# A two-block mixture-of-experts network on one core: tokens gathered from x in fp32 with scaled one-hot columns, expert sums in another slot, and a pair's products in a new order

## The chip, the cores and the metric

The kernel runs on one core of a Trainium2 chip. The metric is the device time of one execution in microseconds (us); lower is better. The core has a matrix engine (TensorE, PE in the profile, with PEld for the loading of its stationary operand), a vector engine (VectorE, DVE), a scalar engine (ScalarE, ACT), GpSimd (POOL), and SyncE (SP), whose queue issues the transfers of weights from HBM into SBUF.

## What is computed

256 tokens of 1024 features go through three layers. Each is a mixer (attention and a recurrence, of different kinds), whose result is added to x, and then a mixture of experts: a router picks a group and two of its eight experts for each token, of 32 in all, and the experts' results are added to x. The change is in the mixture of experts. Cut to what matters, with the grouping of rows left out:

```python
def _hier_moe(h, w_group, b_group, w_expert, b_expert, w1, w3, w2):
    g_sel = jnp.argmax(g_logits, axis=-1)
    top_v, top_i = lax.top_k(e_in, MOE_TOPK)
    gate = (p_g * jax.nn.softmax(top_v, axis=-1)).reshape(-1)
    ids = (g_sel[:, None] * MOE_EXPERTS_PER_GROUP + top_i).reshape(-1)
    ...
    def expert_block(args):
        tok, e = args
        xr = xt[tok]
        return (jax.nn.silu(xr @ w1[e]) * (xr @ w3[e])) @ w2[e]
    ...
    out = jax.ops.segment_sum(y * w_row[:, None], seg, num_segments=N + 1)[:N]

# in the block
h = _rms(x, norm2_w[layer]) * (1 + scale2) + shift2
x = x + gate2 * _hier_moe(h, ...)
```

## The kernel before

x lies in SBUF as two tiles of 128 tokens (NT = 2) by 1024 features in fp32. Feature p*8+k belongs to the k-th of KC = 8 groups, so that `x[:, t].rearrange("q (p k) -> q k p")` reads one group at a step of eight elements.

All weights come through a ring of 19 slots of 1 MB. `plan` queues a weight, `pump` issues its transfer on SyncE as soon as a slot is free beyond a reserve, `done` and `release` give slots back. Parts of the kernel take slots of this ring for themselves: `out_last` (L520), the end of each mixer, takes one for hT, the turned tokens that the router's logits read, and two (hh and hl, L525) for the tokens times their rms factor r, as a high and a low part in fp32r. `token_high` (L557, ScalarE) makes the high part, one operation of 128x1024 per tile, and `token_low` (L561, VectorE) the low part, in halves. At the start of `moe`, hT's slot is given back.

`moe` (L1791) works through 16 pairs of experts, each expert with room for 64 tokens. The program is recorded in the order in which it is written; each engine runs its own instructions in that order and waits on semaphores for the others.

- `onehot(j)` (L1808): for two pairs, u = 1 where a token's rank is a column's number (VectorE).
- `gather(j)` (L1820): xg = the tokens of two pairs. 32 products with hh and hl as the stationary operand and u as the moving one, 256 columns wide; for the first two pairs it is done in two halves of 128 columns. The results leave PSUM by `affine`, by turns on ScalarE and VectorE.
- `gather_w(p)` (L1833): turns the weighted one-hots uw on TensorE; pg and ws are made of them on VectorE.
- `up(p, "g")` and `up(p, "u")` (L1844): 16 products each of xg with the weights. The first ends in sg (ScalarE), the second in hh, the tile of that name in `moe` (VectorE, L1861).
- `turn(p)` (L1866): hh is turned on TensorE, and copied to ht by VectorE (L251).
- `down(p)` (L1889): 16 products of ht with the weights; the result is split in yh and yl.
- `combine(p, t)` (L1902): yh and yl times pg, and VectorE adds the result to x.

Pair p combines the pair before it: one half between up g and up u, the other after the turn. Odd pairs gather for the next two pairs after up u, except pair 5 (LATE), which does so after its down products and combines itself at once. A branch there (`overflow`, L1740) is for experts with more tokens than room, and isn't taken with these inputs. Products that the trace shows twice per instruction are those in fp32.

Of the kernel before, what the change touches and what calls it, by code (L numbers as in the profile page):

```python
# [9 lines left out]
FT = mybir.dt.float32  # L10
# [4 lines left out]
OP = mybir.AluOpType  # L15
# [107 lines left out]
class Net:  # L123
# [396 lines left out]
    def out_last(self, act, gate):  # L520
        got = []
        setup = self.route_setup()
        next(setup)
        self.hT = self.slot().rearrange("p (k q) -> p k q", k=KC)
        self.hs = [self.slot(FR).rearrange("p (t k q) -> p t k q", t=NT, k=KC) for i in range(2)]  # L525
        self.hr = self.cp.tile([P, NT], FT, name="xr", bufs=2)
        for t in range(NT):
            for n in range(2):
                p = self.psum()
                for k2 in range(2):  # L530
                    i = 2 * n + k2
                    if i == len(got):
                        self.prep()
                        got.append(self.ready.pop(0))
                    wh, wl = got[i]
                    for k in range(2):
                        kk = 2 * k2 + k
                        self.mm3(p, tuple(x[:, P * t:P * t + P] for x in act[kk]), (wh[:, k], wl[:, k]), kk == 0, kk == 3)
                    yield (1.3, 0.0)
                self.out_sink(t, n, gate, True)(p)  # L540
                if not t and not n:
                    next(setup)
                if n and not t:
                    self.token_rstd(0)
                    self.token_high(0)
                if t:
                    (self.route_logits if n else self.route_turn)(0)
                    self.token_low(0, 4 * n)
                    yield (1.8, 0.0)
        self.token_rstd(1)  # L550

    def token_rstd(self, t):
        r = self.hr[:, t:t + 1]
        self.nc.vector.tensor_reduce(r, self.ssq[:, t, :2], axis=AX.X, op=OP.add)
        self.rstd(r, r, D)

    def token_high(self, t):  # L557
        xv = self.x[:, t].rearrange("q (p k) -> q k p", k=KC)
        self.nc.scalar.activation(self.hs[0][:, t], xv, AF.Copy, scale=self.hr[:, t:t + 1])

    def token_low(self, t, k):  # L561
        xv = self.x[:, t].rearrange("q (p k) -> q k p", k=KC)
        hh, hl = self.hs
        self.nc.vector.scalar_tensor_tensor(hl[:, t, k:k + 4], xv[:, k:k + 4], self.hr[:, t:t + 1],
                                            hh[:, t, k:k + 4].bitcast(FT), op0=OP.mult, op1=OP.subtract)

    def plan_cols(self, key, w, c0, n):
        src = w.rearrange("(p k) n -> p k n", k=KC)[:, :, c0:c0 + n]
# [1087 lines left out]
    def route(self, g, r, mods, rest):  # L1656
        nc = self.nc
        lg = g.tile([P, NT, 36], FT, name="lg")
        for t in range(NT):
# [34 lines left out]
        rest()  # L1694
# [42 lines left out]
        for i in range(n):  # L1737
            self.mm(p[:, :476], self.ident, self.km, True, True)

    def overflow(self, g, l, h, rk, wt, ti, w1, w3, w2, gate):  # L1740
        nc, tc = self.nc, self.tc
        rv = nc.values_load(ti, min_val=0, max_val=T, skip_runtime_bounds_check_because="rank < T")
        with tc.If(rv >= CAP):  # L1743
# [3 lines left out]
            cnt = g.tile([P, 1], FT, name="top")  # L1747
            nc.vector.memset(cnt, 0.0)
            hT = g.tile([P, KC, T], FT, name="xg")
            for t in range(NT):  # L1750
                for k0 in (0, 4):
                    p = self.psum().rearrange("d (k q) -> d k q", k=4)
                    for k in range(4):
                        for i, part in enumerate(h):
                            self.mm(p[:, k], part[:, t, k0 + k].bitcast(FT), self.ident, i == 0, i == 1)
                    for k in range(4):
                        self.affine(hT[:, k0 + k, P * t:P * t + P], p[:, k], k0 + k, "v")
            with tc.For_i(0, E, 1) as e:
# [7 lines left out]
                with tc.For_i(0, 4, 1) as c:  # L1766
# [12 lines left out]
                    for t in range(NT):  # L1779
                        for n in range(2):  # L1780
                            sl = slice(512 * n, 512 * n + 512)
                            p = self.psum()
                            self.mm(p, ho[:, P * t:P * t + P], wt_[:, sl], True, True)
                            tmp = g.tile([P, 512], FT, name="sg", bufs=2)
                            nc.vector.tensor_scalar(tmp, p, wc[:, t:t + 1], None, op0=OP.mult)
                            if gate:
                                nc.vector.tensor_mul(tmp, tmp, self.ga[:, sl])
                            xs = self.x[:, t, sl]
                            nc.vector.tensor_add(xs, xs, tmp)

    def moe(self, l, mods, start, coeffs, slots, fill=None):  # L1791
        nc, tc = self.nc, self.tc
        _, w1, w3, w2, gate = self.moe_args(l)
        with tc.tile_pool(name="moe", bufs=1, reuse_waits="tile") as g:
            hh, hl = self.hs
            r = self.hr
            self.route_turn(1)
            self.token_high(1)
            self.route_logits(1)
            self.release()  # L1800
            rk, wt, ti, finish, late = self.route(g, r, mods, lambda: self.token_low(1, 0))
            NP = E // 2
            st = {}
            if l == 2:
# [1 line left out]
            bc = lambda a, e, n: a[:, :, e:e + n, None].to_broadcast([P, NT, n, CAP])  # L1806

            def onehot(j):  # L1808
                u = g.tile([P, NT, 4, CAP], FR, name="u", bufs=2)
                nc.vector.tensor_tensor(u, self.iota[:, None, None, :].to_broadcast([P, NT, 4, CAP]), bc(rk, 4 * j, 4),  # L1810
                                        op=OP.is_equal)
                st["u", j] = u

            def weighted(p):
                uw = g.tile([P, NT, 2, CAP], FT, name="uw")
                u = st["u", p // 2][:, :, p % 2 * 2:p % 2 * 2 + 2].bitcast(FT)
                nc.vector.tensor_mul(uw, u, bc(wt, 2 * p, 2))
                st["uw", p] = uw

            def gather(j, c=slice(0, 2 * P)):  # L1820
                if c.start == 0:
                    st["xg"] = g.tile([P, KC, 2 * P], FT, name="xg")
                xg = st["xg"]
                u = st["u", j].rearrange("p t a s -> p t (a s)")
                for k0 in range(0, KC, 2):
                    ps = self.psum().rearrange("p (k s) -> p k s", k=2)[:, :, :c.stop - c.start]
                    for k in range(2):
                        for t in range(NT):
                            for i, part in enumerate((hh, hl)):
                                self.mm(ps[:, k], part[:, t, k0 + k], u[:, t, c], t + i == 0, t + i == 2)  # L1830
                    for k in range(2):
                        self.affine(xg[:, k0 + k, c], ps[:, k], k0 + k, "av"[k])

# [32 lines left out]
            def turn(p):  # L1866
                ps = self.psum()
                for k in range(4):
                    self.tr(ps[:, P * k:P * k + P], st["hh", p][:, k])
                ht = g.tile([P, 512], FT, name="ht").rearrange("p (k s) -> p k s", k=4)  # L1870
                self.copy(ht, ps.rearrange("p (k s) -> p k s", k=4), "v")
                st["ht", p] = ht

            def parts(p, sl, ps):
# [73 lines left out]
            for p in range(NP):  # L1948
                last = p == NP - 1
                if last:  # L1950
                    self.reserve += max(0, slots - 2)
                    if l == 2:
                        fo = self.slot().rearrange("p (t d) -> p t d", t=NT)
                else:
# [27 lines left out]
                (down_last if last else down)(p)  # L1982
                if p == LATE:
                    combine(p, 0)
                    combine(p, 1)
                    self.overflow(g, l, (hh, hl), rk, wt, ti, w1, w3, w2, gate)
                    gather(p // 2 + 1)
                if p == NP - 2:
                    coeffs()
# [81 lines left out]
```

## Time and profile before

| | before |
|---|---|
| median of three runs | 2085.38 us (2081.81 to 2085.57) |
| profiled execution | 2082.4 us, of which the span is 2080.6 us |
| mean granted clock of TensorE | 0.972 |
| TensorE busy | 1885.0 us, 91% |
| weight loads (overlap the products) | 1039.9 us, 50% |
| VectorE busy | 859.2 us, 41% |
| ScalarE busy | 431.3 us, 21% |

The span is one execution, taken by the hardware profiler. The three MoE layers lie at about 228 to 690, 869 to 1331 and 1621 to 2071 us of it; between them lie the mixers. Busy shares are means over stages with different limits. In a row of a group of instructions, `ps<-u,slot 128*128 128x256 f32 x32` means: written tile, read tiles, size of the stationary operand, size of the moving one, and how many.

### The profile page before, as it was taken

Reading aid. Unit: us, or ns where it says so; the run is one execution under the profiler, and the core shown is the slowest. Engines: PE = TensorE matmul, PEld = TensorE weight load, DVE = VectorE, ACT = ScalarE, POOL = GpSimd, SP = SyncE. Lnnn points to the kernel's source line nnn. Section 1 sums busy time; section 2 is a strip of 40 time slices with the busy share of each in tenths; the row PEclk is TensorE's granted clock in tenths of the full one; section 3 lists DMA queues with packets and bytes.
Section 4 is the critical chain, followed back from the end, with each engine's and each line's share of the span. In section 5 each row is a group of like instructions: output and inputs, shape, how many; then the busy total and the mean of one; then the engine's idle time right before and its main releaser. Section 6 shows DMA issues by size and latency. Waiting matters only on the chain. (4 is left out here: it accounts for less than half of the span.)

```text
span 2080.6 us, 25139 instructions
## 1 busy us (share of the span) xinstructions
PE 1885.0 (91%) x10032; PEld 1039.9 (50%) x10032; DVE 859.2 (41%) x1601; ACT 431.3 (21%) x790; POOL 309.6 (15%) x245
## 2 busy tenths in 40 slices
PE   5898899899999889899999999998899999899997
PEld 3656444434444657544343444586788444344443
DVE  3665433323332657633223332367666332222223
ACT  1423211111010333311010111244543111001111
POOL 1331000000000424100000000143443000000000
PEclk8997999999999999999999999899999999999999
DMA  9696999999999966799999999931357999999997
GB/s 322 258 304 236 363 422 422 420 421 421 421 421 406 343 214 247 303 391 421 421 420 421 421 421 421 337 111 41 123 191 270 373 421 421 420 421 421 421 421 270
DMA packets 157542, 725.30 MB, mean 349 GB/s; under 512 B 25305, under 2 KB 43087, under 8 KB 85225
## 3 DMA queue, kind: packets, MB, share of 16 engines
q1 hardware_dynamic: 139216, 716.84, 86.0%
q10 hardware_dynamic: 18201, 6.76, 1.3%
q8 instruction: 82, 1.34, 0.3%
q14 instruction: 43, 0.35, 0.0%
HBM read 722.48 MB, written 1.07 MB: 348 GB/s over the span
## 5 line engine op out<-in xcount | busy, mean ns | idle before, releaser
L258 PE MATMUL ps<-slot,xg 128*64 128x512 f32 x2952 | 680.9, 598 | 0.0
L258 PEld LDWEIGHTS ps<-slot,xg 128*64 128x64 f32 x2952 | 231.0, 138 | 408.7 <-issue 391.7
L258 PE MATMUL ps<-slot,ht 128*64 128x512 f32 (+1 forms) x1592 | 344.8, 574 | 67.6 <-issue 62.9
L258 PE MATMUL ps<-slot 128*128 128x256 f32 (+8 forms) x2230 | 369.9, 326 | 14.0 <-DVE slot L462 9.6
L258 PEld LDWEIGHTS ps<-slot 128*128 128x128 f32 (+3 forms) x2230 | 300.4, 186 | 74.0 <-issue 16.0
L258 PEld LDWEIGHTS ps<-slot,ht 128*64 128x64 f32 x1592 | 130.3, 138 | 257.0 <-issue 244.3
L1908 DVE TENSOR_TENSOR x<-x,ps 128x512 f32<-128x512 f32 x180 | 115.2, 681 | 246.1 <-PE ps L258 246.1
L1882 POOL TENSOR_TENSOR yl<-sg,yh 128x512 fp32r<-128x512 f32 (+1 forms) x68 | 82.4, 1212 | 870.8 <-ACT yh L1881 870.8
L463 POOL TENSOR_TENSOR slot<-slot 128x512 fp32r<-128x512 f32 (+2 forms) x108 | 163.7, 1533 | 282.4 <-ACT slot L461 265.6
L1861 DVE SCALAR_TENSOR_TENSOR hh<-sg,ws,ps 128x512 f32<-128x512 f32 x48 | 53.4, 1113 | 316.5 <-PE ps L258 203.4
L1881 ACT CAST yh<-sg 128x512 fp32r<-128x512 f32 (+1 forms) x68 | 40.3, 593 | 466.1 <-DVE sg L1880 466.1
L462 DVE TENSOR_TENSOR slot<-slot 128x512 fp32r<-128x512 f32 (+2 forms) x108 | 107.4, 1008 | 55.6 <-ACT slot L461 55.1
L1880 DVE TENSOR_TENSOR sg<-ps,ga 128x512 f32<-128x512 f32 (+1 forms) x68 | 44.9, 660 | 178.7 <-PE ps L258 178.7
L258 PEld LDWEIGHTS ps<-u,slot 128*128 128x128 f32 x864 | 104.4, 192 | 23.4 <-issue 17.0
L461 ACT CAST slot<-slot 128x1024 fp32r<-128x1024 f32 (+2 forms) x108 | 106.5, 1020 | 44.8 <-PE ps L258 24.7
L258 PE MATMUL ps<-u,slot 128*128 128x256 f32 (+1 forms) x864 | 109.7, 285 | 3.5 <-DVEq L1743 3.5
L1857 ACT ACTIVATE sg<-ps 128x512 f32<-128x512 f32 x48 | 28.7, 598 | 297.9 <-PE ps L258 297.9
L258 PE MATMUL ps<-yh,pg 128*128 128x512 f32 (+1 forms) x204 | 87.2, 429 | 0.7 <-ACT yh L1881 0.7
L258 PE MATMUL ps<-yl,pg 128*128 128x512 f32 (+1 forms) x204 | 78.5, 387 | 4.3 <-POOL yl L1882 4.0
L399 ACT ACTIVATE xg<-ps,cf 128x256 f32<-128x256 f32 (+1 forms) x72 | 38.9, 540 | 168.0 <-PE ps L258 168.0
L1933 POOL TENSOR_TENSOR slot<-x,rows 128x512 f32<-128x512 f32 x2 | 2.5, 1270 | 463.0 <-DVE x L1929 463.0
L1884 ACT CAST yh<-ps 128x512 fp32r<-128x512 f32 (+1 forms) x34 | 19.0, 560 | 222.7 <-PE ps L258 222.6
(333 smaller groups left out, 1569.3 us busy)
## 6 DMA issues: line engine op xcount, KB each, us to landing
slot<-moe_w SPq DMA_DIRECT2D x376, 1024.0 KB, 17.7
slot<-w_gate SPq DMA_DIRECT2D x59, 1024.0 KB, 19.7
slot<-w_down SPq DMA_DIRECT2D x55, 1024.0 KB, 18.5
slot<-w_up SPq DMA_DIRECT2D x54, 1024.0 KB, 18.8
slot<-ada_w SPq DMA_DIRECT2D x48, 1024.0 KB, 8.8
slot<-w_in SPq DMA_DIRECT2D x20, 1024.0 KB, 5.7
slot<-odd_w_in SPq DMA_DIRECT2D x12, 1024.0 KB, 16.8
more<-w_up SPq DMA_DIRECT2D x10, 1024.0 KB, 16.1
```

The costliest lines, as they stand in the source:

```text
L258: self.nc.tensor.matmul(out, lhsT=lhsT, rhs=rhs, start=start, stop=stop)
L399: self.nc.scalar.activation(out, p, AF.Identity, scale=a, bias=nb[:, k:k + 1])
L461: nc.scalar.copy(wh, src)
L462: nc.vector.tensor_sub(wl[:, 0], src[:, 0], wh[:, 0].bitcast(FT))
L463: nc.gpsimd.tensor_sub(wl[:, 1], src[:, 1], wh[:, 1].bitcast(FT))
L1857: nc.scalar.activation(sg, ps, AF.Silu)
L1861: nc.vector.scalar_tensor_tensor(ha.rearrange("s k p -> s p k"), st["sg", p].rearrange("s (p k) -> s p k", k=4), st["ws", p], ps.rearrange ...
L1880: nc.vector.tensor_mul(y, ps, self.ga[:, sl])
L1881: nc.scalar.copy(yh, y)
L1882: nc.gpsimd.tensor_sub(yl, y, yh.bitcast(FT))
L1884: nc.scalar.copy(yh, ps)
L1908: nc.vector.tensor_add(self.x[:, t, sl], self.x[:, t, sl], ps)
```

## The change

- hh and hl, the slots for them, `token_high` and `token_low` are gone. `gather` has 16 fp32 products with x itself as the stationary operand, read through `xv[:, t, k]` at a step of eight elements, and ur as the moving one: u (now fp32, one buffer) times r, made by ScalarE in `onehot`.
- The expert sums go to acc, which is the slot of hT, kept through the MoE: pair 0 is copied there, pairs 1 to 12 are added there, pairs 13 to 15 to x. Ahead of pair 14 acc is added to x, and its slot is given back.
- In a pair, nothing stands between up g and up u any more. An odd pair gathers, turns, and then combines both halves; an even pair combines one half, turns, and combines the other. gather_w follows. ht is copied by ScalarE.
- `overflow` is adapted to x, r and acc; reserves are adjusted by one slot.

```diff
@@ out_last, token_high, token_low
-        self.hs = [self.slot(FR).rearrange("p (t k q) -> p t k q", t=NT, k=KC) for i in range(2)]
-                    self.token_high(0)
-                    self.token_low(0, 4 * n)
-    def token_high(self, t):
-        xv = self.x[:, t].rearrange("q (p k) -> q k p", k=KC)
-        self.nc.scalar.activation(self.hs[0][:, t], xv, AF.Copy, scale=self.hr[:, t:t + 1])
...
@@ moe
-            hh, hl = self.hs
+            xv = self.x.rearrange("q t (p k) -> q t k p", k=KC)
-            self.token_high(1)
-            self.release()
-            rk, wt, ti, finish, late = self.route(g, r, mods, lambda: self.token_low(1, 0))
+            rk, wt, ti, finish, late = self.route(g, r, mods)
+            acc = self.hT.rearrange("p k q -> p (k q)").rearrange("p (t d) -> p t d", t=NT)
@@ onehot
-                u = g.tile([P, NT, 4, CAP], FR, name="u", bufs=2)
+                u = g.tile([P, NT, 4, CAP], FT, name="u")
+                ur = g.tile([P, NT, 4, CAP], FT, name="ur")
+                for t in range(NT):
+                    nc.scalar.activation(ur[:, t], u[:, t], AF.Copy, scale=r[:, t:t + 1])
@@ gather
-                            for i, part in enumerate((hh, hl)):
-                                self.mm(ps[:, k], part[:, t, k0 + k], u[:, t, c], t + i == 0, t + i == 2)
+                            self.mm(ps[:, k], xv[:, t, k0 + k], u[:, t, c], t == 0, t == NT - 1)
@@ turn
-                self.copy(ht, ps.rearrange("p (k s) -> p k s", k=4), "v")
+                self.copy(ht, ps.rearrange("p (k s) -> p k s", k=4), "a")
@@ combine
-                    nc.vector.tensor_add(self.x[:, t, sl], self.x[:, t, sl], ps)
+                    if p == 0:
+                        nc.vector.tensor_copy(acc[:, t, sl], ps)
+                    else:
+                        to = self.x if p > NP - 4 else acc
+                        nc.vector.tensor_add(to[:, t, sl], to[:, t, sl], ps)
@@ moe, the loop over pairs
-            self.token_low(1, 4)
-                    self.reserve += max(0, slots - 2)
+                    self.reserve += max(0, slots - 1)
+                    if p == NP - 2:
+                        for t in range(NT):
+                            nc.vector.tensor_add(self.x[:, t], self.x[:, t], acc[:, t])
+                        self.release(1, reserve=min(1, slots))
                     up(p, "g")
-                    if p and p - 1 != LATE:
-                        combine(p - 1, 0)
-                    elif not p:
+                    if not p:
                         gather_w(0)
                         start()
                     up(p, "u")
+                    due = p and p - 1 != LATE
                     if not p:
                         gather(0, slice(P, 2 * P))
-                    if p % 2 and p != LATE:
+                    elif p % 2 and p != LATE:
                         gather(p // 2 + 1)
-                        if p == NP - 3:
-                            self.release(2, reserve=min(2, slots))
+                    elif due:
+                        combine(p - 1, 0)
+                    turn(p)
+                    if due:
+                        if p % 2 and p != LATE:
+                            combine(p - 1, 0)
+                        combine(p - 1, 1)
                     gather_w(p + 1)
-                    turn(p)
-                    if p and p - 1 != LATE:
-                        combine(p - 1, 1)
```

An even pair and the gather ahead of it on TensorE, before: `slot,xg` are the up products, `u,slot` the gather, `km,uw` gather_w, `km,hh` the turn, `yh,pg` and `yl,pg` a combine, `slot,ht` the down products.

```order
 L258 MATMUL ps<-yh,pg 128x512
 L258 MATMUL ps<-yl,pg 128x512
 L258 MATMUL ps<-slot,xg 64x512 x16
 L268 MATMUL ps<-km,uw 128x128 x2
 L268 MATMUL ps<-km,hh 128x128 x4
 L258 MATMUL ps<-yh,pg 128x512
 L258 MATMUL ps<-yl,pg 128x512
 L258 MATMUL ps<-yh,pg 128x512
 L258 MATMUL ps<-yl,pg 128x512
 L258 MATMUL ps<-slot,ht 64x512 x16
```

The same place on TensorE now:

```order
 L258 MATMUL ps<-slot,xg 64x512 x32
 L258 MATMUL ps<-yh,pg 128x512
 L258 MATMUL ps<-yl,pg 128x512
 L258 MATMUL ps<-yh,pg 128x512
 L258 MATMUL ps<-yl,pg 128x512
 L268 MATMUL ps<-km,hh 128x128 x4
 L258 MATMUL ps<-yh,pg 128x512
 L258 MATMUL ps<-yl,pg 128x512
 L258 MATMUL ps<-yh,pg 128x512
 L258 MATMUL ps<-yl,pg 128x512
 L268 MATMUL ps<-km,uw 128x128 x2
 L258 MATMUL ps<-slot,ht 64x512 x16
```

The first half of the combine has moved from between the up products to ahead of the turn, and gather_w from ahead of the turn to behind the combine.

The gather at the start of a MoE on TensorE, as the difference of the two programs (`mk,km` are products of the router, `km` alone products whose result isn't read):

```order
 L258 MATMUL ps<-mk,km 128x32 x3
 L258 MATMUL ps<-km 128x476 x2
-L258 MATMUL ps<-u,slot 128x128 x32
+L258 MATMUL ps<-ur,x 128x128 x16
 L258 MATMUL ps<-km,top 1x128
 L258 MATMUL ps<-slot,xg 64x512 x16
```

The place is the same; the operands and the count differ (one fp32 product stands once here and twice in the trace).

ScalarE in an odd pair with a gather, before (L1857 makes sg, L1881 the high part of the down result):

```order
 L1857 ACTIVATE sg<-ps 128x512
 L399 ACTIVATE xg<-ps,cf 128x256 x4
 L1881 CAST yh<-sg 128x512 x2
```

And now:

```order
 L1801 ACTIVATE ur<-u,xr 128x256 x2
 L1846 ACTIVATE sg<-ps 128x512
 L399 ACTIVATE xg<-ps,cf 128x256 x4
 L249 COPY ht<-ps 128x512
 L1870 CAST yh<-sg 128x512 x2
```

The scaling of the one-hots and the copy of ht have come to ScalarE, the copy behind the evictions of the gather.

## Rows read from the trace of the kernel before

**Rows 1.** The page: busy time and share of the engines; transfers in 40 slices.
```profile
PE 1885.0 (91%) x10032; PEld 1039.9 (50%) x10032; DVE 859.2 (41%) x1601; ACT 431.3 (21%) x790; POOL 309.6 (15%) x245
GB/s 322 258 304 236 363 422 422 420 421 421 421 421 406 343 214 247 303 391 421 421 420 421 421 421 421 337 111 41 123 191 270 373 421 421 420 421 421 421 421 270
```

**Rows 2.** Stretches: us, busy PE, PEld, DVE, ACT, POOL, clock, DMA, GB/s.
```profile
228.00:690.00 462.00, 425.92 (x2075) 190.08 (x2073) 142.35 (x233) 51.85 (x94) 41.13 (x34) 0.99 1.00 412
...
1621.00:2071.00 450.00, 417.36 (x2055) 183.58 (x2055) 128.38 (x232) 47.99 (x94) 1.27 (x1) 1.00 0.98 405
```

**Rows 3.** Waits of PEld for weights, 240 to 690: us, times, longest.
```profile
PEld ps L258 <- DMA slot<-moe_w: 1.1, 4, 0.3
```

**Rows 4.** Waits of PE in the third MoE, 1610 to 2075, the largest two.
```profile
PE ps L258 <- issue: 20.9, 14, 1.5
PE ps L268 <- DVE hh L1861: 8.4, 9, 1.3
```

**Rows 5.** Timeline of PE, 1835 to 1895: start, length, group, [idle before].
```profile
1835.08 4.01 PE L258 MATMUL ps<-u,slot 128*128 128x256 f32 x32
1838.92 0.38 PE L268 MATMUL ps<-km,uw 128*128 128x128 f32 x2
...
1842.16 7.09 PE L258 MATMUL ps<-slot,ht 128*64 128x512 f32 x32 [1.49 <-issue]
...
1864.20 0.44 PE L268 MATMUL ps<-km,uw 128*128 128x128 f32 x2
1865.55 0.66 PE L268 MATMUL ps<-km,hh 128*128 128x128 f32 x4 [0.90 <-DVE hh L1861]
...
1868.62 4.05 PE L258 MATMUL ps<-slot,ht 128*64 128x512 f32 x17 [1.49 <-issue]
...
1890.65 4.01 PE L258 MATMUL ps<-u,slot 128*128 128x256 f32 x32
```

**Rows 6.** Timeline of DVE, 1855 to 1872.
```profile
1864.40 1.08 DVE L1861 SCALAR_TENSOR_TENSOR hh<-sg,ws,ps 128x512 f32<-128x512 f32 x1 [6.29 <-issue]
1867.17 0.42 DVE L1839 TENSOR_SCALAR pg<-ps 128x256 fp32r<-128x256 f32 x1 [1.68 <-PE ps L258]
...
1867.84 0.68 DVE L251 COPY ht<-ps 128x512 f32<-128x512 f32 x1
```

**Rows 7.** Weight loads by form: count | busy us, mean ns | idle before.
```profile
L258 PEld LDWEIGHTS ps<-u,slot 128*128 128x128 f32 x864 | 104.4, 192 | 23.4 <-issue 17.0 <-DVEq L1743 5.1 <-DVE u L1810 1.1
L258 PEld LDWEIGHTS ps<-sel,x 128*128 128x128 f32 x96 | 23.3, 335 | 11.5 <-DVE sel L408 6.1 <-issue 5.4
L258 PEld LDWEIGHTS ps<-km,rows 128*128 128x128 f32 x96 | 23.3, 333 | 5.1 <-issue 5.1
```

**Rows 8.** Timeline of PE: 656 to 664, and 690 to 725.
```profile
656.30 3.98 PE L258 MATMUL ps<-km,rows 128*128 128x16 f32 x16
660.21 3.65 PE L258 MATMUL ps<-slot,xg 128*64 128x512 f32 x16
...
696.25 7.43 PE L258 MATMUL ps<-sel,x 128*128 128x128 f32 x30 [0.42 <-DVE sel L408]
703.43 16.60 PE L258 MATMUL ps<-slot 128*128 128x512 f32 x72
```

**Rows 9.** Timeline of PE: half gather (247), and products of 476 columns (1605 to 1622).
```profile
247.55 3.79 PE L258 MATMUL ps<-u,slot 128*128 128x128 f32 x32
251.18 0.40 PE L268 MATMUL ps<-km,uw 128*128 128x128 f32 x2
...
1609.45 4.24 PE L258 MATMUL ps<-km 128*128 128x476 f32 x10
...
1615.13 1.84 PE L258 MATMUL ps<-km 128*128 128x476 f32 x4
```

**Rows 10.** ScalarE by form: count | busy us, mean ns | idle before.
```profile
L1275 ACT ACTIVATE slot<-slot,mx 128x256 f32<-128x256 f32 x16 | 7.9, 496 | 7.3 <-DVE mx L1273 7.3
L249 ACT COPY slot<-ps 128x512 f32<-128x512 f32 x23 | 13.0, 584 | 33.2 <-PE ps L268 18.5 <-PE ps L258 14.7
```

More of the change, by code (lines that the diff above doesn't have):

```diff
@@ L555, in token_rstd @@
         self.rstd(r, r, D)
-    def token_high(self, t):
-        xv = self.x[:, t].rearrange("q (p k) -> q k p", k=KC)
-        self.nc.scalar.activation(self.hs[0][:, t], xv, AF.Copy, scale=self.hr[:, t:t + 1])
-    def token_low(self, t, k):
-        xv = self.x[:, t].rearrange("q (p k) -> q k p", k=KC)
-        hh, hl = self.hs
-        self.nc.vector.scalar_tensor_tensor(hl[:, t, k:k + 4], xv[:, k:k + 4], self.hr[:, t:t + 1],
-                                            hh[:, t, k:k + 4].bitcast(FT), op0=OP.mult, op1=OP.subtract)
     def plan_cols(self, key, w, c0, n):
@@ L1654, in route_logits, with route @@
             self.mm(self.lp[:, t], self.hT[:, k, P * t:P * t + P], self.wr[:, k], k == 0, k == KC - 1)
-    def route(self, g, r, mods, rest):
+    def route(self, g, r, mods):
         nc = self.nc
@@ L1693, in route @@
         nc.vector.tensor_mul(v4(mk), gb, r4(ob))
-        rest()
         p = self.psum((P, NT, E))
@@ L1738, in warm, with overflow @@
             self.mm(p[:, :476], self.ident, self.km, True, True)
-    def overflow(self, g, l, h, rk, wt, ti, w1, w3, w2, gate):
+    def overflow(self, g, l, acc, r, rk, wt, ti, w1, w3, w2, gate):
         nc, tc = self.nc, self.tc
@@ L1749, in overflow @@
             hT = g.tile([P, KC, T], FT, name="xg")
+            xv = self.x.rearrange("q t (p k) -> q t k p", k=KC)
             for t in range(NT):
+                dg = g.tile([P, 512], FT, name="sg", bufs=2)[:, :P]
+                nc.vector.tensor_scalar(dg, self.ident, r[:, t:t + 1], None, op0=OP.mult)
                 for k0 in (0, 4):
@@ L1753, in overflow @@
                     for k in range(4):
-                        for i, part in enumerate(h):
-                            self.mm(p[:, k], part[:, t, k0 + k].bitcast(FT), self.ident, i == 0, i == 1)
+                        self.mm(p[:, k], xv[:, t, k0 + k], dg, True, True)
                     for k in range(4):
@@ L1787, in overflow @@
                                 nc.vector.tensor_mul(tmp, tmp, self.ga[:, sl])
-                            xs = self.x[:, t, sl]
+                            xs = acc[:, t, sl]
                             nc.vector.tensor_add(xs, xs, tmp)
@@ L1794, in moe @@
         with tc.tile_pool(name="moe", bufs=1, reuse_waits="tile") as g:
-            hh, hl = self.hs
             r = self.hr
+            xv = self.x.rearrange("q t (p k) -> q t k p", k=KC)
             self.route_turn(1)
-            self.token_high(1)
             self.route_logits(1)
-            self.release()
-            rk, wt, ti, finish, late = self.route(g, r, mods, lambda: self.token_low(1, 0))
+            rk, wt, ti, finish, late = self.route(g, r, mods)
+            acc = self.hT.rearrange("p k q -> p (k q)").rearrange("p (t d) -> p t d", t=NT)
             NP = E // 2
@@ L1808, in onehot @@
             def onehot(j):
-                u = g.tile([P, NT, 4, CAP], FR, name="u", bufs=2)
+                u = g.tile([P, NT, 4, CAP], FT, name="u")
                 nc.vector.tensor_tensor(u, self.iota[:, None, None, :].to_broadcast([P, NT, 4, CAP]), bc(rk, 4 * j, 4),
                                         op=OP.is_equal)
-                st["u", j] = u
+                ur = g.tile([P, NT, 4, CAP], FT, name="ur")
+                for t in range(NT):
+                    nc.scalar.activation(ur[:, t], u[:, t], AF.Copy, scale=r[:, t:t + 1])
+                st["u", j], st["ur", j] = u, ur
             def weighted(p):
                 uw = g.tile([P, NT, 2, CAP], FT, name="uw")
-                u = st["u", p // 2][:, :, p % 2 * 2:p % 2 * 2 + 2].bitcast(FT)
+                u = st["u", p // 2][:, :, p % 2 * 2:p % 2 * 2 + 2]
                 nc.vector.tensor_mul(uw, u, bc(wt, 2 * p, 2))
@@ L1823, in gather @@
                 xg = st["xg"]
-                u = st["u", j].rearrange("p t a s -> p t (a s)")
+                u = st["ur", j].rearrange("p t a s -> p t (a s)")
                 for k0 in range(0, KC, 2):
@@ L1985, in moe @@
                     combine(p, 1)
-                    self.overflow(g, l, (hh, hl), rk, wt, ti, w1, w3, w2, gate)
+                    self.overflow(g, l, acc, r, rk, wt, ti, w1, w3, w2, gate)
                     gather(p // 2 + 1)
```

## The prediction

> **What bounds the kernel now.** I read the page first, then the waits of TensorE, then the order of events over two neighbouring pairs of experts, and last the costs by form of the operations that the change swaps. On the page TensorE is busy for 91% of the span, and in long stretches the transfers run at a flat 421 GB/s [rows 1]. Those stretches are the three MoE layers, 462 us in the first and 450 us in the third, and TensorE is busy for over nine tenths of them [rows 2]. Two things could set the pace there, TensorE or the weights; the waits decide. Over most of the first MoE the weight loads of TensorE waited for a moe_w transfer 4 times, 1.1 us in all [rows 3]: the transfers keep just ahead. TensorE's own waits are larger: 14 of about 1.5 us (20.9 us) that the profile calls issue, and 9 waits for hh (8.4 us) [rows 4]. So a MoE is a string of products on TensorE with about 29 us of holes, and the change is judged on that string: what it adds to the products, what it takes out of the holes.
>
> The holes are seen in two pairs of the third MoE, from 1835.08 to 1890.65, 55.6 us [rows 5]. The 1.49 us stands ahead of each pair's down products (1842.16, 1868.62). It ends when ht has been copied. On VectorE that copy stands behind pg and ws, and pg at 1867.17 waits for TensorE's last combine product, so that ht starts only at 1867.84 and the products follow 0.78 us later [rows 6]. In an even pair there is also 0.90 us ahead of the turn (1865.55), while hh is made from 1864.40 on; in an odd pair the gather stands there and covers it.
>
> **What the new order takes away.** ht is copied by ScalarE, whose nearest copy of the same shape takes 584 ns [rows 10]; nothing stands between it and the turn but evictions that are due earlier. Half a combine is about 1.2 us of products: the hole begins at 1868.62 - 1.49 = 1867.13, 1.6 us after the turn's start, and the turn is some 0.4 of that [rows 5]. Both halves, or one, and gather_w (0.4 us) now stand between turn and down and cover the copy. In even pairs one half of the combine stands ahead of the turn: about 1.2 us against the 1.35 us from the end of up u (1864.20) to the turn (1865.55) [rows 5]; some 0.1 us stays. Pair 6 has no combine left and keeps both holes. So 13 of the 14 waits of 1.49 us go (19.4 us), and 8 of the 9 for hh (7.5 us, the eighth in pair 0, where the second half of the first gather now stands). Together **-26.8 us per MoE**. The combine products themselves are only moved.
>
> **What the new gather costs.** The number of instructions stays: 32 of fp32r before (high and low part of the tokens, two tiles, eight k), after it 16 products in fp32, which the trace counts twice. What differs is the stationary operand. Before it is a contiguous slice of hh or hl, after it x[:, t] read at every eighth element, 32 bytes apart. Before knows that reading in two places, the turning of x (sel,x) and km,rows: their weight loads take 335 and 333 ns where the loads for the gather take 192 [rows 7], all 128x128. What counts is the pace: 30 products with sel,x from 696.25 to 703.43 are 0.239 us each, and 16 with km,rows from 656.30 to 660.21 are 0.244, although those have 16 columns only [rows 8]. So the columns don't set this pace, the load does. The gather of before runs at 3.84 / 32 = 0.120 (1835.08 to 1838.92) [rows 5], and the half gather at 3.63 / 32 = 0.113 [rows 9].
> The fp32 columns could be slower than the load: 476 columns take (4.24 - 1.84) / 6 = 0.400 us [rows 9], so 256 take 0.215 and 128 take 0.108. Both are under 0.239, and I take the load. A full gather then costs 31 x 0.239 + 0.215 = 7.6 us against 3.84, +3.75 us; a half gather about 7.5 against 3.63, +3.85. Each MoE has seven full ones (pairs 1, 3, 7, 9, 11, 13, and after the late pair 5) and two halves: 26.25 + 7.7, **+34.0 us per MoE**. All of it is on TensorE's string; what used to be covered by the odd pair's gather (hh) was covered by the short one too.
> [...]
>
> **The start of a MoE and the small parts.** The scaled one-hots ur are two activations of 128x256 on ScalarE, nearest row 496 ns [rows 10], between u and the first gather: +1.0 us once. For later gathers they are made two up products (14 us) ahead and cost nothing. token_high and token_low leave ScalarE and VectorE, where next to nobody waited for them; ahead of the layer the copy of the turned tokens stood behind token_high, and I credit an estimated 0.5 us, about one such copy. The copies of pair 0, the addition of acc to x ahead of pair 14 (two operations of 128x1024 on VectorE, which has 7 us until hh) and the swapped targets of the additions lie beside TensorE; without that cover the addition would cost 2 to 3 us per MoE once. Two ring slots come free and one is kept through the MoE, so weights may start one slot (about 2.5 us at 421 GB/s) earlier. As TensorE becomes slower, the transfers gain on it: nothing to win, nothing to lose. The mixers' products keep their order.
>
> **Sum.** Per MoE 34.0 - 26.8 + 1.0 - 0.5 = +7.7 us, three times +23 us. If the last product of a gather lies beside the next load, each gather is some 0.13 us shorter, 1.1 per MoE, and the sum +20. The profiled execution took 2082.4 us, 3.0 below the median of 2085.38 and inside the runs' 2081.81 to 2085.57. It would become 2102 to 2105, the median 2105 to 2108. I say **2106 us**.
>
> **The rivals.**
> (A) The full gather hides the load. If the load overlaps the 256 columns better than the 128 of sel,x, the full gather runs at the columns' 0.215: 32 x 0.215 = 6.9, +3.0 instead of +3.75. That takes 5.2 us off per MoE: +2.5, three times +7.5, about 2092. At its best, with the start free too, 2089. For it: 0.239 and 0.215 are close. Against it: two rows with different columns show the same pace.
> (B) The other side, faster. Were the load of x no slower than that of a contiguous slice, halves would cost nothing more (0.108 per product) and full gathers +3.0: 21.0 - 26.8 + 0.5 = -5.3 per MoE, -16, about 2069. The point from which it decides: the gathers may add no more than 26.3 us per MoE, a pace of 0.21 us. The transfers, just ahead of TensorE now, would then keep some of it. Against it stand both rows of the strided reading, 0.239 and 0.244; only a load that goes faster where x has just been written, or beside other moving data, would give it.
> [...]
> (C) A hole stays. If ht on ScalarE comes behind the last eviction of xg and the casts, or hh is later than the one combine half, the even pairs keep one wait: 8 x 0.93 = 7.5 us per MoE, +22, about 2128. For it: the evictions of a gather alternate between ScalarE and VectorE. Against it: they end before the turn, and 584 ns stand against 1.6 us of products.
> (D) Load and product don't overlap fully at 256 columns. At the load's own 335 ns per product a gather would be 10.7 us, seven times +3.1 per MoE more, about 2170; at 0.27, +1.0 each, about 2127. Against it: contiguous loads hide whole behind 476 columns.
> That the slices of x aren't read at the step is excluded by the code: x is kept as token by feature, and feature p*8+k belongs to k.
>
> **How the numbers follow.** The forecast (load sets the pace, holes go) 0.73, 2096 to 2116; A 0.10; B 0.08; C 0.05; D 0.04. The range reaches down to A's 2089 and up to C's 2128 and leaves out B and the far part of D. A measurement here can tell 0.2%, 4.2 us, from no change. Faster by more than that: B and a little of the rest, 0.09. Within: half of A and a little of B, 0.06. Slower: 0.85.
>
> **What would show it.** In the profile after: weight loads with ur,x at about 333 ns; full and half gathers both near 7.5 us; no issue waits of 1.49 but one (pair 6) per MoE; waits for hh of 0.1 to 0.2 us in even pairs; two pairs at 55.6 - 1.5 - 2.4 + 3.75 = 55.4 us in the middle of the layer; each MoE longer by some 7 us, and the mixers unchanged. [...] It is wrong if the pace of ur,x is under 0.22 or over 0.26, or if a new wait for ht, xg or a transfer appears.

## The result and the profile after

The changed kernel takes 2098.94 us (median of four runs, 2097.55 to 2100.18) against 2085.48 beside it: a ratio of 1.0066 with a 95% interval of 1.0049 to 1.0084, 13.5 us slower. Forecast were 2106 us, between 2089 and 2128, and slower. The profiled execution here took 2100.18 us, the slowest of the four, and that of before 2082.4 us, near its fastest, so their spans lie further apart, 2098.4 against 2080.6 us, 17.8 us.

The page of the changed kernel: busy time and share of the engines.

```profile
PE 1980.8 (94%) x10032; PEld 1118.1 (53%) x10032; DVE 819.8 (39%) x1547; ACT 466.7 (22%) x880; POOL 311.4 (15%) x245
```

Beside [rows 1]: TensorE issues as many instructions as before and is busy for 96 us more; its weight loads take 78 us more.

The weight loads of the changed kernel by form (count | busy us, mean ns | idle before):

```profile
L258 PEld LDWEIGHTS ps<-ur,x 128*128 128x128 f32 x864 | 208.8, 336 | 24.9 <-issue 20.5 <-ACT ur L1801 2.9 <-DVEq L1729 1.5
```

Beside [rows 7]: 864 loads as before, 336 ns in the place of 192. That is the duration of the two strided readings that the kernel had already.

TensorE's waits of the changed kernel from 1560 to 2100, which holds the third MoE (us in total, times, longest):

```profile
PE ps L268 <- DVE hh L1850: 3.7, 9, 1.3
PE ps L258 <- ACT ht L249: 1.7, 3, 0.7
```

Beside [rows 4]: the 14 waits called issue (20.9 us) are gone, and those for hh have shrunk from 8.4 to 3.7 us. The short ones for ht are as large as before: three of 1.7 us in all, where before had two of 1.6. So both halves of the change did what the code says, the loss and the gain.

Two pairs of the third MoE on TensorE, in the changed kernel (start, length, group, [idle before]); the same two pairs as in [rows 5]:

```profile
1853.53 8.04 PE L258 MATMUL ps<-ur,x 128*128 128x256 f32 x32
1861.41 0.60 PE L268 MATMUL ps<-km,hh 128*128 128x128 f32 x4
1863.69 0.38 PE L268 MATMUL ps<-km,uw 128*128 128x128 f32 x2
1864.00 7.09 PE L258 MATMUL ps<-slot,ht 128*64 128x512 f32 x32
1870.92 13.90 PE L258 MATMUL ps<-slot,xg 128*64 128x512 f32 x64
...
1886.13 0.66 PE L268 MATMUL ps<-km,hh 128*128 128x128 f32 x4 [0.17 <-DVE hh L1850]
1887.55 0.38 PE L268 MATMUL ps<-km,uw 128*128 128x128 f32 x2
1887.87 3.65 PE L258 MATMUL ps<-slot,ht 128*64 128x512 f32 x16
...
1908.62 3.73 PE L258 MATMUL ps<-ur,x 128*128 128x256 f32 x14
```

The gather lasts from 1853.53 to 1861.41, 7.88 us in the place of 3.84. The down products follow gather_w without a hole, and the turn waits 0.17 us for hh instead of 0.90. Two pairs take 1908.62 - 1853.53 = 55.09 us; before, 55.57. The gain of the order and the loss of the gather cancel almost exactly over such pairs, and what is left is mainly the two half gathers, the gather after the late pair, and the start.

ScalarE in the odd one of these pairs: the last eviction of the gather, and the copy of ht.

```profile
1861.61 0.47 ACT L397 ACTIVATE xg<-ps,cf 128x256 f32<-128x256 f32 x1 [1.45 <-PE ps L258]
1862.10 0.58 ACT L249 COPY ht<-ps 128x512 f32<-128x512 f32 x1
```

ht is there at 1862.68, before gather_w starts on TensorE at 1863.69. In [rows 6] it was copied 3.44 us after hh was begun, behind pg.

### The profile page after: what moved, and what is told of

Its sections match the earlier page's. It is cut to its first block, busy times and chain, and to the rows that moved or that the text cites. A ratio compares the mean times of both kernels' runs of the same rounds, so it can differ in the third digit from the quotient of the medians.

```text
span 2098.4 us, 25180 instructions
## 1 busy us (share of the span) xinstructions
PE 1980.8 (94%) x10032; PEld 1118.1 (53%) x10032; DVE 819.8 (39%) x1547; ACT 466.7 (22%) x880; POOL 311.4 (15%) x245
## 3 DMA queue, kind: packets, MB, share of 16 engines
q8 instruction: 81, 1.33, 0.3%
## 5 line engine op out<-in xcount | busy, mean ns | idle before, releaser
L258 PE MATMUL ps<-slot,xg 128*64 128x512 f32 x2992 | 662.4, 599 | 0.0
L258 PEld LDWEIGHTS ps<-slot,xg 128*64 128x64 f32 x2992 | 215.3, 138 | 430.0 <-issue 419.9
L258 PE MATMUL ps<-slot,ht 128*64 128x512 f32 (+1 forms) x1552 | 327.8, 575 | 4.9 <-ACT ht L249 4.9
L258 PEld LDWEIGHTS ps<-ur,x 128*128 128x128 f32 x864 | 208.8, 336 | 24.9 <-issue 20.5
L258 PE MATMUL ps<-ur,x 128*128 128x256 f32 (+1 forms) x864 | 216.1, 408 | 4.3 <-DVEq L1729 3.7
L258 PEld LDWEIGHTS ps<-slot,ht 128*64 128x64 f32 x1552 | 108.2, 139 | 190.2 <-issue 176.6
L1901 DVE TENSOR_TENSOR slot<-slot,ps 128x512 f32<-128x512 f32 x144 | 90.7, 680 | 5.7 <-PE ps L258 3.8
L403 DVE TENSOR_SCALAR xg<-ps,cf 128x256 f32<-128x256 f32 (+1 forms) x72 | 37.0, 514 | 110.7 <-ACT xg L399 110.7
L249 ACT COPY ht<-ps 128x512 f32<-128x512 f32 x48 | 28.0, 584 | 224.8 <-PE ps L268 224.6
```

Of the source, the lines that this page charges most:

```text
L258: self.nc.tensor.matmul(out, lhsT=lhsT, rhs=rhs, start=start, stop=stop)
L403: self.nc.vector.tensor_scalar(out, p, a, nb[:, k:k + 1], op0=OP.mult, op1=OP.add)
L1901: nc.vector.tensor_add(to[:, t, sl], to[:, t, sl], ps)
```

## The experiments

All runs compute the whole network. The first four take the change apart: order and gather each alone, and the copy of ht on either engine under either order.

**The new gather alone.** The loop over pairs is that of before, and ht is copied by VectorE:

```diff
-                self.copy(ht, ps.rearrange("p (k s) -> p k s", k=4), "a")
+                self.copy(ht, ps.rearrange("p (k s) -> p k s", k=4), "v")
@@ the loop: combine(p - 1, 0) between up g and up u, gather_w ahead of turn,
@@ combine(p - 1, 1) behind it, as before
```

> The new gather, acc and ur alone; the order of a pair and the copy of ht by VectorE as before. Theory (the strided weight load sets the gather's pace at 0.239 us a product): +34 to +36 us per MoE, about 2190 us, with the 14 waits of 1.5 us and the 9 waits for hh unchanged. Rival (the gather costs its columns only, and the time after the change came from something in the new order): full gathers +3.0, halves nothing, about +22 per MoE, 2150 us.

Measured: 2190.73 us (2190.32 to 2196.68), ratio 1.0511 (1.0493 to 1.0529). TensorE's waits from 225 to 700, and the two pairs of the third MoE:

```profile
PE ps L258 <- issue: 21.0, 14, 1.6
PE ps L268 <- DVE hh L1850: 7.2, 8, 0.9
```

```profile
1925.08 8.05 PE L258 MATMUL ps<-ur,x 128*128 128x256 f32 x32
...
1936.21 7.09 PE L258 MATMUL ps<-slot,ht 128*64 128x512 f32 x32 [1.49 <-issue]
...
1959.59 0.66 PE L268 MATMUL ps<-km,hh 128*128 128x128 f32 x4 [0.90 <-DVE hh L1850]
...
1962.67 3.65 PE L258 MATMUL ps<-slot,ht 128*64 128x512 f32 x16 [1.49 <-issue]
...
1984.71 5.64 PE L258 MATMUL ps<-ur,x 128*128 128x256 f32 x22
```

The holes are those of before (the ninth wait for hh lies behind this window; over the span both kernels have 27, 25.5 us in all), and two pairs take 59.63 us, 4.06 more than before. By the medians the gather costs 104.7 us, 34.9 for each MoE; the rival, by columns, gave 65 in all. These totals include the mixers. From the router's first products to the first products behind the MoE (in the third to the end of the span), the three MoEs are 34.2, 38.1 and 38.7 us longer in the profile than before, and the first of them starts 5.9 us earlier. So the loss is that of the prediction in kind, and a little larger.

**The new gather, old order, ht by ScalarE.** One letter against the run above:

```diff
-                self.copy(ht, ps.rearrange("p (k s) -> p k s", k=4), "v")
+                self.copy(ht, ps.rearrange("p (k s) -> p k s", k=4), "a")
```

> As the run with the new gather alone, but ht copied by ScalarE; the order of a pair is that of before. Theory (the hole of 1.5 us is the queue on VectorE, where the copy stands behind pg, and pg waits for the combine): the copy's engine alone takes out the 1.5 us, the waits for hh stay, 8 x 0.93 = 7.4 us per MoE more than the changed kernel, about 2121 us. Rival (the hole needs the new order, more products between turn and down): most of the 1.5 us stays, 2170 to 2190 us.

Measured: 2128.36 us (2122.71 to 2131.03), ratio 1.0202 (1.0181 to 1.0223). The same pairs:

```profile
1874.80 8.05 PE L258 MATMUL ps<-ur,x 128*128 128x256 f32 x32
...
1884.36 7.09 PE L258 MATMUL ps<-slot,ht 128*64 128x512 f32 x32
...
1907.73 0.66 PE L268 MATMUL ps<-km,hh 128*128 128x128 f32 x4 [0.90 <-DVE hh L1850]
1909.26 3.65 PE L258 MATMUL ps<-slot,ht 128*64 128x512 f32 x16
...
1931.30 3.97 PE L258 MATMUL ps<-ur,x 128*128 128x256 f32 x15
```

The wait ahead of the down products is gone with the engine of one copy, 62 us in all; the 0.90 us for hh stays. Two pairs take 56.50 us, 3.13 less.

**The changed kernel with ht copied by VectorE.** The same letter, under the new order.

> The changed kernel with the copy of ht given back to VectorE; the new order stays, so that the copy stands ahead of pg in VectorE's queue. Theory (the queue behind pg was the cause, not the engine's speed): 2099 to 2104 us, the combine covers the copy. Rival (VectorE itself is too slow or too busy with the additions): the waits of about 1 us come back ahead of the down products, 13 per MoE, about 2140 us.

Measured: 2103.87 us (2103.13 to 2105.29), ratio 1.0087; the interval (1.0071 to 1.0104) overlaps that of the changed kernel. Of the 42 waits called issue that the kernel before has over the span, this is left:

```profile
PE ps L258 <- issue: 2.8, 3, 1.0
```

So either edit alone removes the 1.5 us: another engine, or a place ahead of pg in VectorE's queue. The cause of the hole was the queue: the copy stood behind pg, and pg behind the combine on TensorE that was meant to cover the copy.

What the new order gives beyond that is 2128.36 - 2098.94 = 29 us, where the prediction had 22 for the wait for hh. Only half of the 29 is that wait. Over the span, with the old order and with the new one (both with ht on ScalarE):

```profile
PE ps L268 <- DVE hh L1850: 25.6, 27, 1.3
```

```profile
PE ps L268 <- DVE hh L1850: 11.3, 27, 1.3
```

The rest is in no row of waits. In the two pairs shown, 56.50 - 55.09 = 1.41 us, the wait for hh is 0.73. Another 0.30 is in the up products: with nothing between them they take 13.83 us in a pair (1870.92 to 1884.75), with half a combine between them 6.96 + 7.02. The last 0.38 lies where the products of the combine now follow one another.

**The new order alone**, with the gather, hh, hl and sums of before:

```diff
-                self.copy(ht, ps.rearrange("p (k s) -> p k s", k=4), "v")
+                self.copy(ht, ps.rearrange("p (k s) -> p k s", k=4), "a")
@@ the loop over pairs as in the changed kernel, with
+                        if p == NP - 3:
+                            self.release(2, reserve=min(2, slots))
```

> The kernel before with the new order of a pair and ht copied by ScalarE; gather from the high and low parts as before, sums into x. Theory for TensorE alone: 26.8 us less per MoE, which would be 2005 us. But the weights came only just ahead before (transfers at a flat 421 GB/s), so I expect TensorE to wait for moe_w now, and a gain of 3 to 6 us per MoE only: 2068 to 2076 us, with waits for moe_w of some 20 us per MoE. Rival (the weights have room): 2005 to 2020 us and no such waits.

Measured: 2073.51 us (2072.63 to 2075.54), ratio 0.9941 (0.9924 to 0.9958). The largest wait of TensorE over the whole span, and full gathers early and late in the first MoE:

```profile
PE ps L258 <- DMA slot<-moe_w: 34.5, 32, 1.3
```

```profile
270.94 4.00 PE L258 MATMUL ps<-u,slot 128*128 128x256 f32 x32
322.01 4.04 PE L258 MATMUL ps<-u,slot 128*128 128x256 f32 x32
...
488.79 4.01 PE L258 MATMUL ps<-u,slot 128*128 128x256 f32 x32
548.72 4.01 PE L258 MATMUL ps<-u,slot 128*128 128x256 f32 x32
608.34 4.01 PE L258 MATMUL ps<-u,slot 128*128 128x256 f32 x32
```

Early, two pairs take 51.07 us, 4.50 less than the 55.57 before; the prediction's terms made 3.9 of it. Late they take 59.6 to 59.9 us, longer than before. That is the pace of the weights: two pairs read 24 slots of 1 MB, which at 421 GB/s [rows 1] take 24 x 2.49 = 59.8 us. The 80 us that TensorE alone was to gain become 12.5 us, since the pairs ran off the stock in the ring and then waited for moe_w. TensorE waited for its weights 16.5 us in the first MoE, 17.9 in the second, and 17.6 in the third, whose weights have other names in the rows (w_gate, w_up and more): near the 20 expected.

**The step of the stationary operand.** These four kernels have the new order, unscaled one-hots, sums into x, and one fp32 copy of x, scaled by r, in a ring slot. They differ in one number: how far apart the 128 columns of a stationary operand lie in the copy (and, with it, in how many operations ScalarE makes the copy).

```diff
-        self.hs = [self.slot(FR).rearrange("p (t k q) -> p t k q", t=NT, k=KC) for i in range(2)]
+        self.hs = self.slot().rearrange("p (t c) -> p t c", t=NT)
+    def token_part(self, t, k):
+        a, s = k // STEP, k % STEP
+        return self.hs[:, t, P * STEP * a:P * STEP * a + P * STEP].rearrange("q (p s) -> q s p", s=STEP)[:, s]
-                            for i, part in enumerate((hh, hl)):
-                                self.mm(ps[:, k], part[:, t, k0 + k], u[:, t, c], t + i == 0, t + i == 2)
+                            self.mm(ps[:, k], self.token_part(t, k0 + k), u[:, t, c], t == 0, t == NT - 1)
```

Columns contiguous:

> New order of a pair, ht by ScalarE; the gather in fp32 from one scaled copy of x in a ring slot (made by ScalarE in the place of the high part), unscaled one-hots, sums into x, no acc. The copy is laid out so that the 128 columns of a stationary operand are contiguous. Theory (the step of 32 bytes slows the load): loads of about 190 ns, full gathers at the columns' 0.215 us a product (6.9 us), halves at 0.12 (3.8): some 13 us per MoE less on TensorE than in the changed kernel, of which the weights let through a part; 2066 to 2078 us with waits for moe_w. Rival (fp32 operands load slowly however they lie): 2095 to 2100 us, loads of 335 ns.

Two elements apart, four, and eight:

> The same with columns two elements (8 bytes) apart. [...] Rival (any step costs, or cost grows with the step): loads between 190 and 335 ns.

> The same with columns four elements (16 bytes) apart. [...] Rival (cost grows with the step): loads clearly under 335 ns.

> The same kernel with one number changed: the columns of a stationary operand lie eight elements (32 bytes) apart in the copy, as they do in x. Theory: loads of 335 ns, gathers of 7.6 us, the time of the changed kernel or 1 to 3 us per MoE less (no ur ahead of the first gather), 2090 to 2099 us. Rival (what costs is reading x itself, not the step): the time of the contiguous copy.

Measured: 2064.86 us for contiguous columns (2061.91 to 2067.47, ratio 0.9901, 0.9875 to 0.9926), 2062.54 and 2092.67 for a step of two and of four (one run each), and 2095.72 for eight (2095.46 to 2098.33, ratio 1.0052, 1.0034 to 1.0071). The first is 1 us below the range expected for it. Their weight loads for the gather, in the order of the step:

```profile
L258 PEld LDWEIGHTS ps<-u,slot 128*128 128x128 f32 x864 | 149.3, 192 | 39.9 <-issue 17.0 <-DVEq L1739 4.8 <-DVE u L1804 1.1
```

```profile
L261 PEld LDWEIGHTS ps<-u,slot 128*128 128x128 f32 x864 | 155.0, 198 | 36.6 <-issue 17.0 <-DVEq L1744 5.1 <-DVE u L1809 1.1
```

```profile
L261 PEld LDWEIGHTS ps<-u,slot 128*128 128x128 f32 x864 | 205.2, 328 | 24.2 <-issue 17.0 <-DVEq L1744 4.8 <-DVE u L1809 1.1
```

```profile
L261 PEld LDWEIGHTS ps<-u,slot 128*128 128x128 f32 x864 | 209.2, 337 | 23.0 <-issue 17.0 <-DVEq L1744 4.8 <-DVE u L1809 1.1
```

192, 198, 328, 337 ns: the cost hardly grows from 4 to 8 bytes and from 16 to 32, and jumps between 8 and 16. So the rival at four, loads clearly under 335 ns, fell; of the range of the rival at two, 190 to 335, only the lower end came, 6 ns above the contiguous load. Why the jump lies between 8 and 16 bytes no run shows. That x itself is read has no part in it: at a step of eight the copy loads as slowly as x (337 and 336 ns). The full and the half gather with contiguous columns, and at a step of eight:

```profile
243.18 3.84 PE L258 MATMUL ps<-u,slot 128*128 128x128 f32 x32
246.85 0.60 PE L268 MATMUL ps<-km,hh 128*128 128x128 f32 x4
...
268.88 7.17 PE L258 MATMUL ps<-u,slot 128*128 128x256 f32 x32
275.89 0.60 PE L268 MATMUL ps<-km,hh 128*128 128x128 f32 x4
```

```profile
247.44 7.95 PE L261 MATMUL ps<-u,slot 128*128 128x128 f32 x32
255.22 0.60 PE L271 MATMUL ps<-km,hh 128*128 128x128 f32 x4
277.24 8.05 PE L261 MATMUL ps<-u,slot 128*128 128x256 f32 x32
285.13 0.60 PE L271 MATMUL ps<-km,hh 128*128 128x128 f32 x4
```

The half gather falls from 7.78 to 3.67 us, the full one only from 7.89 to 7.01: contiguous, its 256 columns in fp32 set the pace (7.01 / 32 = 0.219), no longer the load. Between contiguous columns and a step of eight lie 30.9 us, from this one number. With contiguous columns the kernel is 1% faster than before and 1.6% faster than the changed one.

**What the ring's depth is worth.** The contiguous kernel has longer gathers on TensorE than the one with only the order changed (7.01 us against 3.84), and is faster by 8.6 us. It holds one ring slot through the MoE where that one holds two. So one more slot was taken, with nothing in it:

```diff
+        self.idle = self.slot()
+        self.nc.vector.memset(self.idle[:, :1], 0.0)
@@ pair 13
+                            nc.vector.memset(self.idle[:, :1], 0.0)
-                            self.release(1, reserve=min(1, slots))
+                            self.release(2, reserve=min(2, slots))
```

> The kernel with the contiguous copy, and one ring slot more that is taken at the end of the mixer and touched again by VectorE at pair 13, so that it is lost to the weights as in the kernel before. Theory (the ring's depth is why this kernel, with more work on TensorE than the one with only the order changed, is faster): the weights come one slot, 2.5 us, later; 2068 to 2073 us, and the waits for moe_w rise from 2.6 and 2.9 us per MoE to about 5. Rival (the weights don't limit it): 2063 to 2067 us, waits as they were.

Measured: 2072.1 us (2068.01 to 2078.08), 7.2 us more by the medians, but the span of the profile was only 2.0 us longer: it shows the fastest of the four runs. Both were run again side by side:

> The kernel with the contiguous copy again, on one chip with the next run, in more rounds, since the cost of the ring slot was 7 us by the medians and 2 us by the spans of the profiles. Theory: 2062 to 2067 us.

> The same with the ring slot taken. Theory (one slot is 2.5 us per MoE): 5 to 8 us more than the run beside it. Rival (by the profiles' spans): 0 to 3 us more.

Measured: 2064.28 us (ratio 0.9903, 0.9887 to 0.9919) and 2076.92 us (ratio 0.9954, 0.9938 to 0.9971). One slot costs 12.6 us by the medians of these runs and 7.2 by those of the first, where 5 to 8 were expected (2.5 per MoE); the sign is settled, the size isn't. The waits of TensorE's weight loads for moe_w over the span, without the slot taken and with it:

```profile
PEld ps L258 <- DMA slot<-moe_w: 10.4, 11, 2.2
```

```profile
PEld ps L258 <- DMA slot<-moe_w: 17.8, 20, 2.2
```

In these two profiles, 12.0 us apart, the three MoEs are 4.3, 3.3 and 4.0 us longer, each in its later pairs: up to the fifth full gather of the first MoE (491 us) the two kernels keep step to 0.02 us. Some 4 us appear between the last full gather of the first MoE and the first gather of the next, half of them in the mixer, where the granted clock from 690 to 860 is 0.91 instead of 0.94. Why a slot costs more than the 2.5 us per MoE wasn't tried. With the same two slots held, the contiguous kernel and the one with only the order changed come to about the same time (2072.1 or 2076.92, and 2073.51), as one would expect of two kernels that wait for the same transfers.

**The copy in the slot of the turned tokens**, after the logits, so that no second slot is taken at the end of the mixer:

```diff
-        self.hs = self.slot().rearrange("p (t c) -> p t c", t=NT)
-                    self.token_high(0)
-            self.token_high(1)
             self.route_logits(1)
-            self.release()
+            self.hs = self.hT.rearrange("p k q -> p (k q)").rearrange("p (t c) -> p t c", t=NT)
+            self.token_high(0)
+            self.token_high(1)
```

> The kernel with the contiguous copy, made in the slot of the turned tokens after the logits, while the router runs on VectorE (some 7 us in which ScalarE is idle; the two operations take 4.5), so that no second slot is taken at the end of the mixer. Theory: the copy is hidden, the weights start up to one slot earlier, 2058 to 2064 us. Rival (the copy, now wholly behind the logits, delays the first gather): up to 2 us per MoE more, 2066 to 2071 us.

Measured: 2063.51 us (2057.13 to 2066.76), ratio 0.9883 (0.9859 to 0.9906). The copy is hidden: among the waits of TensorE that the profile lists from 850 to 1340 and from 1595 to 2075, down to 0.4 and 0.2 us, none is for it. But the interval overlaps that of the contiguous kernel (0.9875 to 0.9926), so nothing is shown to be gained.

## Why the prediction was right

- **The bound.** TensorE's string of products and holes sets the MoE; every run with the new gather showed it. The waits of its weight loads for moe_w over the span, 1.9 us before and 2.2 in the changed kernel, stayed small until TensorE became faster (10.4 us in the contiguous kernel).
- **The gather (+34.0 per MoE)** was the step that decided the sign, and its mechanism held: 336 ns for a load, and a pace set by the load. The pace was 7.88 / 32 = 0.246 us instead of 0.239. So +4.04 per full gather, not +3.75; the half gather in pair 0 took 7.71 (+4.08, not +3.85). Seven and two of these are 36.4 per MoE, 2.4 more than forecast.
- **The holes (-26.8 per MoE)** came to more: 2190.73 - 2098.94 = 91.8 us, 30.6 per MoE. The prediction had the wrong pairs. The 14 waits called issue are those of pairs 0 to 5 and 7 to 14; the wait of pair 6, the one it left standing, was never among them. Ahead of the down products of pairs 0 and 6, before:

```profile
253.65 7.09 PE L258 MATMUL ps<-slot,ht 128*64 128x512 f32 x32 [1.62 <-issue]
...
426.97 7.09 PE L258 MATMUL ps<-slot,ht 128*64 128x512 f32 x32 [0.78 <-DVE ht L251]
```

  and of pair 0 in the changed kernel:

```profile
256.75 3.65 PE L258 MATMUL ps<-slot,ht 128*64 128x512 f32 x16 [0.46 <-ACT ht L249]
```

  So all 14 went, with 0.46 us left in pair 0, and pair 6's fell to 0.46 as well. Of the waits for hh the eighth that went was pair 5's, since pair 0 had none; pair 6's grew from 0.91 to 1.29 us, because gather_w no longer stands ahead of its turn. Together the waits for hh fell by 4.7 us per MoE, not 7.5. The waits thus give 25.5 of the 30.6; the other 5 are in no wait. Two pairs shrank by 59.63 - 55.09 = 4.54 us, and the waits shown in them by 2 x 1.49 + 0.73 = 3.71. The rest is in holes a little longer than their 1.49 us (two of them went with 3.13) and in products that follow one another more closely, for which the prediction had no term: to it, the combine products "themselves are only moved".
- **The two together.** The even pair gained 2.6 instead of 2.4, the odd one lost 2.1 instead of 2.25; two pairs took 55.09 us, not 55.4. Over six and a half such couples that is 2 us per MoE, 6 of the 7 us by which 2106 was too high. That the sum came so near is in part luck: the loss was 2.4 us per MoE too small, the gain 3.8.
- **The start (+1.0)** was a little over half that. The first product waited only 0.20 us for ur, the rest lay behind products whose result isn't read; from the router's products to the first gather it took 2.70 us against 2.10:

```profile
216.46 0.83 PE L258 MATMUL ps<-mk,km 128*128 128x32 f32 x6 [0.42 <-DVE mk L1680]
...
219.16 7.88 PE L258 MATMUL ps<-ur,x 128*128 128x128 f32 x32 [0.20 <-ACT ur L1801]
```

  The 0.5 credited ahead of it is there in two of three MoEs: from the first turn of the tokens to the router's products it took 0.6 us less in the first and second, and 0.1 more in the third.
- **The granted clock** moved in both directions; the sum has no term for it. Two windows of before, and the same of after (us, busy engines, then clock, DMA share, GB/s):

```profile
404.00:408.00 4.00, 3.84 (x18) 3.84 (x19) 0.54 (x1) 0.58 (x2) 0.00 (x0) 0.50 1.02 416
660.00:664.00 4.00, 4.00 (x19) 1.45 (x19) 0.40 (x3) 0.00 (x0) 0.00 (x0) 1.00 1.01 421
```

```profile
404.00:408.00 4.00, 4.00 (x18) 4.00 (x18) 0.54 (x1) 0.74 (x2) 0.00 (x0) 1.00 1.01 410
660.00:664.00 4.00, 4.00 (x12) 1.17 (x10) 0.00 (x1) 0.00 (x0) 0.00 (x0) 0.50 1.02 424
```

  0.50 is the lowest clock that either trace shows in windows of 1 us. At 404, behind the late pair, TensorE had been idle for 1.33 us before and for 1.42 us after, and only before did the clock fall: that gather took 6.13 us. At 660 the fall came without a pause: since 647 TensorE had waited for nothing, and 16 up products took 6.24 us instead of 3.65. So of these falls one came behind a pause and one without, and of two like pauses one brought none. Over the span the mean clock is 0.971 against 0.972, so it nearly cancels.
- **The MoEs and the mixers.** From the router's first products to the first products behind the MoE (in the third to the end of the span), the three MoEs took 7.4, 7.7 and 4.5 us more, where some 7 were forecast for each. "The mixers unchanged" was wrong: the first ended 3.4 us earlier (granted clock 0.96 against 0.93 from 50 to 100, and 0.80 against 0.77 from 150 to 200), the second took 2.3 us longer.
- **The rivals.** A (full gather at the pace of its columns, 0.215) fell with 0.246. B, the other side, fell with the 336 ns; a kernel near to it, the one with the contiguous copy and without ur and acc, took 2064.86 us, where I had 2069. C fell: the turn waits 0.17 us. D, a partly exposed load, would have begun at 0.27; at most the step from 0.239 to 0.246 is of that kind.

## What to carry to other kernels

Before a copy into a better layout is taken away, look in the trace for a place that already reads the operand in the raw layout, and take the pace of its products, not their columns; here sel,x showed 0.239 us a product before anything ran, and the gather then took 0.246. A wait that the profile puts down to issue may be a copy queued behind an operation that waits for the very work meant to cover it (here 14 waits of some 1.5 us in a MoE), and moving that copy to another engine is the cheapest test (62 us less by that alone). When TensorE gets faster than the weights arrive, the gain lasts only as long as the stock in the ring (here 12.5 of 80 us came), so one slot (7.2 and 12.6 us) was worth more here than the products that a shorter gather saves (with two slots held in both, the kernel with the shorter one took 1.4 us more or 3.4 less).

## What the hardware showed that I had not expected

In the four steps tried, the load of 128 fp32 columns has two costs: 192 and 198 ns at steps of 4 and 8 bytes, 328 and 337 ns at 16 and 32. A step of two is nearly free (the full gather takes 7.02 us against 7.01, the half gather 3.87 against 3.67, in one run), so here a layout could interleave two groups at almost no cost (2062.54 us against 2064.86). And the idle ring slot, which moves no data, cost 7 to 13 us, where one slot at the weights' pace in each MoE would be 7.5.
